# Odd chunks with hi and lo in each other's tile, so that successive moving operands of TensorE alternate between two offsets

## The chip, the core and the metric

The kernel runs on one core of a Trainium2 chip. The metric is the device time of one execution in microseconds (us), the median of several runs. TensorE is called PE here, VectorE DVE, ScalarE ACT, GpSimd POOL and SyncE SP, as in the profile.

## What is computed

Two layers of a diffusion backbone on 256 latent and 256 context tokens with 1024 features. Each layer is a gated feed-forward half step (FFN), a mixing step with four branches on one input projection, and a second FFN. Cut to what matters here:

```python
def ffn_half(z, shift, scale, gate, norm, wg, wu, wd):
    return z + 0.5 * gate * swiglu(modulate(rmsnorm(z, norm), shift, scale), wg, wu, wd)

def swiglu(z, wg, wu, wd):
    return (jax.nn.silu(z @ wg) * (z @ wu)) @ wd          # 1024 -> 2816 -> 1024

def merge_branches(branches, gate_pre, w_branch, w_out):
    gates = jax.nn.sigmoid(gate_pre).reshape(..., N_BRANCH, D_MODEL)
    merged = gates[..., 0, :] * (branches[0] @ w_branch[0])
    for n in range(1, N_BRANCH):
        merged = merged + gates[..., n, :] * (branches[n] @ w_branch[n])
    return merged @ w_out

for l in range(2):                                        # x: latent tokens, h: context tokens
    x = ffn_half(x, ...ffn1...); h = ffn_half(h, ...ffn1...)
    y, y_c = token_mixing(modulate(rmsnorm(x)), modulate(rmsnorm(h)), w_in[l], ...)
    x = x + mod[5] * y
    x = ffn_half(x, ...ffn2...)
    if l == 0: h = ffn_half(h + mod_c[5] * y_c, ...ffn2...)
return rmsnorm(x, final_norm)
```

All matrices are f32. The output is the latent stream, 256 x 1024.

## The kernel before

Activations lie with the features on the 128 partitions and the tokens along the free dimension: a tensor of 1024 features is 8 chunks of 128 partitions x 512 tokens (latent 0 to 255, context 256 to 511). Weights come in units of 128 x 1024 (8 blocks of 128 x 128).

Every large product is made of three fp32r matmuls. A value is split into hi, its fp32r rounding, and lo, the rest (`split`, L81 on ACT for hi, L84 on DVE for lo), and the product is hi x hi + hi x lo + lo x hi. `mm3` does this for a chunk k: L110 takes the weights' hi and the activations' hi, L111 the weights' hi and the activations' lo, L112 the weights' lo and the activations' hi. The activations are the moving operand (512 columns, or 256 where one half of the tokens is worked on), the weights the stationary one, loaded anew for each matmul. So the moving operands of a row of chunks run hi, lo, hi, hi, lo, hi. `group` (L123 to L125) does the same for several outputs side by side in the order hi, hi, lo, at the beginning of a phase. `proj_tok` (L615 to L617) has the activations as stationary operand.

The activations' parts lie in these tiles:

- `xs`, one tile for the whole kernel, holds hi (`xh`) and lo (`xl`) of the normed input of the current phase, 8 chunks of 2048 bytes a partition each. `place` puts them there by the table `PLACES`, in f32 elements: start of hi, distance of lo, and offsets `off` for the tiles below. In layer 0 and in the first FFN of layer 1 hi starts 60 elements into the tile and lo 8 x 512 + 32 further; as built, hi stands at 112 and lo at 240 bytes modulo 256. In the mixing and the second FFN of layer 1 the distance is 8 x 512, and both stand at 192.
- `hh` and `hl`, the FFN's hidden layer, 11 chunks of 2048 bytes each for one half of its 22 (`hidden`, by `off`): 112 and 240 modulo 256 in the same phases, both at 192 in the second FFN of layer 1.
- `bh` and `bl`, a branch's output (2 chunks), 112 and 240 in layer 0, one common offset in layer 1.
- `mh` and `ml`, the merged branches (8 chunks), at the beginning of their tiles: both at 0 in layer 0, both at 192 in layer 1.

The weight tiles `whi` and `wlo` stand at 0 modulo 256 nearly everywhere. The outputs' names tell the places: `pg` and `pu` are the FFN's first products, `pd` its second (11 chunks an output), `last` the last two outputs of a second product, made for 256 tokens at a time, `proj` the input projections, `gate` and `pb` the branches' gates and projections in `merge`, `po` the product with `w_out`, `mm`, `aux` and `first` those of `group`.

The tile framework sets each engine's order from the order in the code and from priorities; DMAs are issued by SP. A weight unit is loaded into `raw`, cast by ACT (`whi`), subtracted by DVE (`wlo`) and used by PE. In the last layer `early` (L396, L397) fills two columns of `xs` with the shift of the second FFN, hi by ACT and lo by DVE, while `merge` ends and `po` begins.

Of the kernel before, what the change touches and what calls it, by code (L numbers as in the profile page):

```python
# [10 lines left out]
F32 = mybir.dt.float32  # L11
F32R = mybir.dt.float32r
U8 = mybir.dt.uint8
AF = mybir.ActivationFunctionType
ALU = mybir.AluOpType
AX = mybir.AxisListType

P = 128
L = 2
D = 1024  # L20
NK = D // P
T = 256
TT = 2 * T
# [3 lines left out]
FH = NFC // 2  # L27
# [18 lines left out]
LINE = 32  # L46
# [2 lines left out]
PLACES = {(0, C_N1): (60, NK * TT + LINE, (28, 12)), (0, C_NM): (60, NK * TT + LINE, ((28, 60), (28, 60))),  # L49
          (0, C_N2): (60, NK * TT + LINE, (28, 12)), (1, C_N1): (60, NK * TT + LINE, (28, 12)),  # L50
          (1, C_NM): (80, NK * TT, ((0, 0), (64, 64))), (1, C_N2): (80, NK * TT, (112, 0))}


def ada_chunks(s):
# [4 lines left out]
class Net:  # L59
    def __init__(self, ctx, tc, ins, out):  # L60
        self.ctx, self.tc, self.nc, self.i, self.out = ctx, tc, tc.nc, ins, out
        self.n = 0
        pool = lambda name, **kw: ctx.enter_context(tc.tile_pool(name=name, **kw))
        self.cp = pool("const", bufs=1)
        self.wp = pool("weights", bufs=4)
        self.tp = pool("temps", bufs=2)
        self.ps = pool("psum", bufs=1, space=bass.MemoryType.PSUM)
        self.fill = self.apool = None
        self.steady, self.due = False, 0.0
# [113 lines left out]
    def place(self, l, phase):  # L183

        h, d, o = PLACES[l, phase]
        self.xh, self.xl = (self.xs[:, a:a + NK * TT].rearrange("p (k t) -> p k t", t=TT) for a in (h, h + d))
        return o

    def half(self):
# [199 lines left out]
    def early(self, l):  # L389


        nc = self.nc
        g = self.gain(l, 7, C_N2)
        sh = self.mods(l, 6)
        hi = self.xh[:, :, T - 2:T]
        nc.scalar.copy(hi, sh)  # L396
        nc.vector.tensor_tensor(out=self.xl[:, :, T - 2:T], in0=sh, in1=hi.bitcast(F32), op=ALU.subtract)  # L397
        return g

    def early_chunk(self, g, m):  # L400
# [65 lines left out]

    def hidden(self, hp, off):

        return tuple(hp.tile([P, FH * TT + pad], F32R, tag=t, name=t)[:, a:a + FH * TT].rearrange(
            "p (f t) -> p f t", t=TT) for t, pad, a in zip(("hh", "hl"), (112, 16), off))  # L470

    def cold_units(self, wgu, hp, evac, off):

# [369 lines left out]
    def mix(self, l, segs):  # L843
        nc, tc, i = self.nc, self.tc, self.i
# [3 lines left out]
        off = self.place(l, C_NM)  # L848
        with tc.tile_pool(name=f"mix{l}", bufs=1) as mp:
# [7 lines left out]
            turn = 1  # L857

            def branch():
                nonlocal turn  # L860
                turn = 1 - turn
                pair = [mp.tile([P, 2 * TT + 2 * LINE], F32R, tag=t, bufs=2, name=t) for t in ("bh", "bl")]
                return tuple(t[:, a:a + 2 * TT].rearrange("p (c t) -> p c t", t=TT) for t, a in zip(pair, off[turn]))

            def merge(b, bo, first=False):

                for m in range(NK):
                    if m % 4 == 0:
                        w = self.unit(i["wbr"][l, b, m // 4])
                    ps = self.mm("gate")  # L870
                    self.mm3(ps[:, :n], self.unit(i["wgate"][l, b, m]), self.xh, self.xl, range(NK), 0, n)
                    g = mp.tile([P, TT], F32, tag="g", bufs=2, name="g")
                    nc.scalar.activation(g[:, :n], ps[:, :n], AF.Tanh, scale=0.5)
                    ps = self.mm("pb")
                    self.mm3(ps[:, :n], w, bo[0], bo[1], (0, 1), 0, n, k0=2 * (m % 4))
                    t = acc[:, m, :n] if first else g[:, :n]
                    nc.vector.scalar_tensor_tensor(out=t, in0=g[:, :n], scalar=1.0, in1=ps[:, :n],
                                                   op0=ALU.add, op1=ALU.mult)
                    if not first:
                        nc.vector.tensor_tensor(out=acc[:, m, :n], in0=acc[:, m, :n], in1=t, op=ALU.add)  # L880
                    yield m
# [98 lines left out]
            with tc.tile_pool(name=f"br{l}", bufs=1) as bp:  # L980
# [66 lines left out]

                rounds(recurrence(0, obs))
                bc = branch()
                rounds(pooling(bc), "B")  # L1050
                ba = branch()
                rounds(attention_a(ba), "B")
                rounds(self.proj_tok(l, U_BI, bv))
                rounds(merge(2, bc, first=True))
                drain("B")
                rounds(recurrence(1, obs))
                drain("A")
                bd = branch()
                rounds(attention_d(bd))
                rounds(merge(0, ba))  # L1060
# [3 lines left out]
                bb = branch()  # L1064
                rounds(readout(bb))
            with tc.tile_pool(name=f"mg{l}", bufs=1) as gp:
                mh = gp.tile([P, NK, TT], F32R, tag="mh", name="mh")
                ml = gp.tile([P, NK, TT], F32R, tag="ml", name="ml")
                for m in merge(1, bb):
                    self.split(acc[:, m, :n], mh[:, m, :n], ml[:, m, :n])  # L1070
                gate = self.gate(l, 5)
                self.fresh(segs)
                g = self.early(l) if ns == 1 else None

                def out(m, ps, c0, c1, mid=iter(()), ws=[None] * NK):
                    if ws[m] is None:
                        ws[m] = self.unit(i["wout"][l, m], NK * P, *((gp, 2) if m >= NK - 2 else ()))
                    self.mm3(ps, ws[m], mh, ml, range(3), c0, c1, last=False)
                    next(mid, None)
                    self.mm3(ps, ws[m], mh, ml, range(3, 6), c0, c1, first=False, last=False, k0=3)  # L1080
                    next(mid, None)
                    self.mm3(ps, ws[m], mh, ml, range(6, NK), c0, c1, first=False, k0=6)

                for m in range(NK - 2):
                    ps = self.mm("po")
                    out(m, ps[:, :n], 0, n)
                    for r in segs:
                        self.update(ps, m, gate, r, r * T, True)
                    if g is not None:
                        self.early_chunk(g, m)  # L1090
                self.last_chunks(out, gate, segs, g)
# [163 lines left out]
```

## Time and profile before

| | us |
|---|---|
| median of 3 runs | 2109.31 |
| lowest and highest run | 2108.45, 2116.08 |
| the profiled execution | 2115.61 |
| its span, first to last instruction | 2113.8 |
| PE busy in it | 2087.5 |
| DVE busy | 1434.9 |
| ACT busy | 904.5 |

The granted clock of PE was 0.998 over the span. A row of a group of instructions names line, engine, operation, output and inputs, shape and count, then the busy time in us and the mean length of one in ns, then the idle time before them. A row of the timeline begins with the start in us from the span's start and the length in us. The ends of matmuls are modelled, and matmuls overlap; their starts are measured.

### The profile page before, as it was taken

The numbers are of one execution on the slowest core, as the hardware profiler recorded it, in microseconds if no ns is written. First come the engines' busy times: TensorE is split into PE (matmuls) and PEld (weight loads), VectorE is DVE, ScalarE is ACT, GpSimd is POOL, SyncE is SP. The second block draws the span as 40 slices with busy tenths as digits, with TensorE's granted clock in tenths as the row PEclk, the third lists the DMA queues.
The fourth block names the chain that finished last, engine by engine and source line by source line (L and its number), as shares of the span: only waits on it lengthen the run. The fifth ranks groups of instructions, "written<-read, shape, count | busy, mean of one in ns | idle before, by whom it ended". The sixth has DMA issues, their size and how long they took to land.

```text
span 2113.8 us, 31650 instructions
## 1 busy us (share of the span) xinstructions
PE 2087.5 (99%) x12446; PEld 1801.0 (85%) x12446; DVE 1434.9 (68%) x2355; ACT 904.5 (43%) x1488; POOL 39.4 (2%) x95
## 2 busy tenths in 40 slices
PE   8999999999999999999999999999999999999998
PEld 5888888988888888988888898888889989999998
DVE  5988986676366455676676667667666858677555
ACT  3332333547446433433233343223335655666443
POOL 0000000001000000000000000000000000000000
PEclk9999999999999999999999999999999999999999
DMA  7655654221222222344454334345443233455553
GB/s 304 216 175 188 215 186 140 96 98 51 75 76 80 71 97 98 110 143 138 144 183 157 124 128 161 130 156 173 146 128 114 98 120 110 141 184 181 176 189 116
DMA packets 89509, 296.71 MB, mean 140 GB/s; under 512 B 10256, under 2 KB 12176, under 8 KB 89360
## 3 DMA queue, kind: packets, MB, share of 16 engines
q1 hardware_dynamic: 89360, 294.69, 41.4%
q8 instruction: 98, 1.61, 0.3%
q14 instruction: 51, 0.42, 0.1%
HBM read 293.60 MB, written 1.05 MB: 139 GB/s over the span
## 4 chain that ended last, share of the span: by engine, by line
PE 94%; DVE 2%; ACT 2%; issue 1%; DMA 0%; DVEq 0%; ACTq 0%; SPq 0%
PE pg L110 6%; PE pu L110 6%; PE pg L112 6%; PE pu L112 6%; PE pg L111 6%; PE pu L111 6%; PE pd L110 6%; PE pd L112 6%; PE pd L111 6%; PE gate L112 4%; PE gate L110 4%; PE gate L111 4%; PE proj L111 2%; PE proj L110 2%; PE proj L112 2%; PE blev L777 2%
## 5 line engine op out<-in xcount | busy, mean ns | idle before, releaser
L81 ACT CAST whi<-raw 128x1024 fp32r<-128x1024 f32 (+2 forms) x444 | 430.7, 972 | 827.4 <-PE pu L111 200.3
L84 DVE TENSOR_TENSOR wlo<-raw,whi 128x1024 fp32r<-128x1024 f32 (+2 forms) x444 | 498.2, 1123 | 289.3 <-ACT whi L81 282.5
L285 DVE SCALAR_TENSOR_TENSOR aacc<-araw,sil,aacc 128x512 f32<-128x512 f32 x448 | 312.5, 745 | 122.0 <-DMA araw<-in_wada 121.6
L112 PE MATMUL pg<-xs,wlo 128*128 128x512 f32 (+1 forms) x640 | 233.0, 364 | 0.0
L112 PE MATMUL pu<-xs,wlo 128*128 128x512 f32 (+1 forms) x640 | 233.0, 364 | 0.0
L110 PE MATMUL pg<-xs,whi 128*128 128x512 f32 (+1 forms) x640 | 232.5, 363 | 0.4 <-ACT xs L376 0.4
L110 PE MATMUL pu<-xs,whi 128*128 128x512 f32 (+1 forms) x640 | 232.3, 363 | 0.0
L111 PE MATMUL pg<-xs,whi 128*128 128x512 f32 (+1 forms) x640 | 231.4, 362 | 0.0
L111 PE MATMUL pu<-xs,whi 128*128 128x512 f32 (+1 forms) x640 | 231.3, 361 | 0.0
L112 PE MATMUL pd<-hh,wlo 128*128 128x512 f32 (+1 forms) x616 | 224.3, 364 | 0.0
L110 PE MATMUL pd<-hh,whi 128*128 128x512 f32 (+1 forms) x616 | 223.8, 363 | 0.0
L111 PE MATMUL pd<-hl,whi 128*128 128x512 f32 (+1 forms) x616 | 222.7, 361 | 0.0
L110 PE MATMUL gate<-xs,whi 128*128 128x512 f32 (+1 forms) x512 | 172.5, 337 | 0.0
L112 PE MATMUL gate<-xs,wlo 128*128 128x512 f32 (+1 forms) x512 | 171.7, 335 | 0.0
L111 PE MATMUL gate<-xs,whi 128*128 128x512 f32 (+1 forms) x512 | 170.8, 334 | 0.0
L110 PEld LDWEIGHTS pg<-xs,whi 128*128 128x128 f32 x640 | 120.8, 189 | 20.8 <-issue 1.8
L110 PEld LDWEIGHTS pu<-xs,whi 128*128 128x128 f32 x640 | 120.8, 189 | 20.1 <-issue 2.0
L111 PEld LDWEIGHTS pu<-xs,whi 128*128 128x128 f32 x640 | 120.2, 188 | 19.4
L111 PEld LDWEIGHTS pg<-xs,whi 128*128 128x128 f32 x640 | 120.2, 188 | 19.4
L112 PEld LDWEIGHTS pg<-xs,wlo 128*128 128x128 f32 x640 | 120.1, 188 | 18.5
L112 PEld LDWEIGHTS pu<-xs,wlo 128*128 128x128 f32 x640 | 120.1, 188 | 18.5
L110 PEld LDWEIGHTS pd<-hh,whi 128*128 128x128 f32 x616 | 116.2, 189 | 19.5 <-issue 2.2
(278 smaller groups left out, 3794.5 us busy)
## 6 DMA issues: line engine op xcount, KB each, us to landing
raw<-in_wgu SPq DMA_DIRECT2D x176, 512.0 KB, 4.0
araw<-in_wada SPq DMA_DIRECT2D x128, 512.0 KB, 3.3
raw<-in_wgate SPq DMA_DIRECT2D x64, 512.0 KB, 3.2
raw<-in_wd SPq DMA_DIRECT2D x64, 384.0 KB, 3.1
raw<-in_win SPq DMA_DIRECT2D x44, 512.0 KB, 3.3
raw<-in_wd SPq DMA_DIRECT2D x64, 320.0 KB, 2.8
aspace<-in_wada SPq DMA_DIRECT2D x16, 512.0 KB, 8.9
raw<-in_wbr SPq DMA_DIRECT2D x16, 512.0 KB, 3.3
```

The costliest lines, as they stand in the source:

```text
L81: nc.scalar.copy(hi, src)
L84: nc.vector.tensor_tensor(out=lo, in0=src, in1=hi.bitcast(F32), op=ALU.subtract)
L110: nc.tensor.matmul(ps, wh, a, start=first and j == 0, stop=False)
L111: nc.tensor.matmul(ps, wh, b, start=False, stop=False)
L112: nc.tensor.matmul(ps, wl, a, start=False, stop=last and j == n - 1)
L285: nc.vector.scalar_tensor_tensor(out=acc[r], in0=w[:, j], scalar=c, in1=acc[r], op0=ALU.mult, op1=ALU.add)
L777: nc.tensor.matmul(ps[:, g * P:(g + 1) * P], k[:, h, g * P:(g + 1) * P], x[:, h, (g ^ cross) * P:((g ^ cross) + 1) * P], start=True, stop= ...
```

## The change

A new class `Chunks` holds two views of one shape and gives, for chunk i, the first where i is even and the second where it is odd. `parts(a, b)` makes two of them, with the views in one order and in the other. `place`, `hidden` and `branch` return such pairs, so that hi of an odd chunk lies where its lo lay, and lo where hi lay. `mh` and `ml` become such a pair too, and their tiles are 64 elements longer, with the offsets `off[0]` inside. `early`, which wrote all chunks in one instruction, writes even and odd chunks apart.

```diff
--- before.py
+++ after.py
@@ -49,6 +49,20 @@
 PLACES = {(0, C_N1): (60, NK * TT + LINE, (28, 12)), (0, C_NM): (60, NK * TT + LINE, ((28, 60), (28, 60))),
           (0, C_N2): (60, NK * TT + LINE, (28, 12)), (1, C_N1): (60, NK * TT + LINE, (28, 12)),
           (1, C_NM): (80, NK * TT, ((0, 0), (64, 64))), (1, C_N2): (80, NK * TT, (112, 0))}
+
+
+class Chunks:
+
+    def __init__(self, even, odd):
+        self.turns = (even, odd)
+
+    def __getitem__(self, i):
+        return self.turns[i[1] % 2][i]
+
+
+def parts(a, b):
+
+    return Chunks(a, b), Chunks(b, a)
 
 
 def ada_chunks(s):
@@ -183,7 +197,7 @@
     def place(self, l, phase):
 
         h, d, o = PLACES[l, phase]
-        self.xh, self.xl = (self.xs[:, a:a + NK * TT].rearrange("p (k t) -> p k t", t=TT) for a in (h, h + d))
+        self.xh, self.xl = parts(*(self.xs[:, a:a + NK * TT].rearrange("p (k t) -> p k t", t=TT) for a in (h, h + d)))
         return o
 
     def half(self):
@@ -392,9 +406,10 @@
         nc = self.nc
         g = self.gain(l, 7, C_N2)
         sh = self.mods(l, 6)
-        hi = self.xh[:, :, T - 2:T]
-        nc.scalar.copy(hi, sh)
-        nc.vector.tensor_tensor(out=self.xl[:, :, T - 2:T], in0=sh, in1=hi.bitcast(F32), op=ALU.subtract)
+        for j in range(2):
+            hi, lo = (x.turns[j][:, j::2, T - 2:T] for x in (self.xh, self.xl))
+            nc.scalar.copy(hi, sh[:, j::2])
+            nc.vector.tensor_tensor(out=lo, in0=sh[:, j::2], in1=hi.bitcast(F32), op=ALU.subtract)
         return g
 
     def early_chunk(self, g, m):
@@ -466,8 +481,8 @@
 
     def hidden(self, hp, off):
 
-        return tuple(hp.tile([P, FH * TT + pad], F32R, tag=t, name=t)[:, a:a + FH * TT].rearrange(
-            "p (f t) -> p f t", t=TT) for t, pad, a in zip(("hh", "hl"), (112, 16), off))
+        return parts(*(hp.tile([P, FH * TT + pad], F32R, tag=t, name=t)[:, a:a + FH * TT].rearrange(
+            "p (f t) -> p f t", t=TT) for t, pad, a in zip(("hh", "hl"), (112, 16), off)))
 
     def cold_units(self, wgu, hp, evac, off):
 
@@ -860,7 +875,7 @@
                 nonlocal turn
                 turn = 1 - turn
                 pair = [mp.tile([P, 2 * TT + 2 * LINE], F32R, tag=t, bufs=2, name=t) for t in ("bh", "bl")]
-                return tuple(t[:, a:a + 2 * TT].rearrange("p (c t) -> p c t", t=TT) for t, a in zip(pair, off[turn]))
+                return parts(*(t[:, a:a + 2 * TT].rearrange("p (c t) -> p c t", t=TT) for t, a in zip(pair, off[turn])))
 
             def merge(b, bo, first=False):
 
@@ -1064,8 +1079,8 @@
                 bb = branch()
                 rounds(readout(bb))
             with tc.tile_pool(name=f"mg{l}", bufs=1) as gp:
-                mh = gp.tile([P, NK, TT], F32R, tag="mh", name="mh")
-                ml = gp.tile([P, NK, TT], F32R, tag="ml", name="ml")
+                mh, ml = parts(*(gp.tile([P, NK * TT + 2 * LINE], F32R, tag=t, name=t)[:, a:a + NK * TT].rearrange(
+                    "p (k t) -> p k t", t=TT) for t, a in zip(("mh", "ml"), off[0])))
                 for m in merge(1, bb):
                     self.split(acc[:, m, :n], mh[:, m, :n], ml[:, m, :n])
                 gate = self.gate(l, 5)
```

Nothing moves on PE. In the second product of a first FFN (`pd`, layer 0; `hh` and `hl` are the two tiles, `whi` and `wlo` the weights' parts) the rows of PE before are these, three for a chunk, from an odd chunk on:

```order
L110 MATMUL pd<-hh,whi 128x512
L111 MATMUL pd<-hl,whi 128x512
L112 MATMUL pd<-hh,wlo 128x512
L110 MATMUL pd<-hh,whi 128x512
L111 MATMUL pd<-hl,whi 128x512
L112 MATMUL pd<-hh,wlo 128x512
```

and now, in the same place:

```order
L124 MATMUL pd<-hl,whi 128x512
L125 MATMUL pd<-hh,whi 128x512
L126 MATMUL pd<-hl,wlo 128x512
L124 MATMUL pd<-hh,whi 128x512
L125 MATMUL pd<-hl,whi 128x512
L126 MATMUL pd<-hh,wlo 128x512
```

In the odd chunk the two tiles have changed places, and no two rows that follow each other read the same one.

On ACT, where the last branch is merged in layer 1 and `po` begins (`g` is the Tanh of a gate, `mh` and `ml` the cast of a merged chunk, `whi` that of a weight unit, `xs<-mod_93` the copy in `early`), the rows before are:

```order
L81 CAST mh<-macc 128x256
L81 CAST whi<-raw 128x1024
L873 ACTIVATE g<-gate 128x256
L396 CAST xs<-mod_93 128x8x2
L81 CAST whi<-raw 128x1024
L81 CAST mh<-macc 128x256
```

and now:

```order
L95 CAST mh<-macc 128x256
L411 CAST xs<-mod_93 128x4x2
L95 CAST whi<-raw 128x1024
L888 ACTIVATE g<-gate 128x256
L411 CAST xs<-mod_93 128x4x2
L95 CAST whi<-raw 128x1024
L95 CAST ml<-macc 128x256
```

The copy of the even chunks stands one weight cast and one gate earlier than the whole copy stood; that of the odd chunks stands where it was. On DVE at the same place before:

```order
L84 TENSOR_TENSOR ml<-macc,mh 128x256
L84 TENSOR_TENSOR wlo<-raw,whi 128x1024
L877 SCALAR_TENSOR_TENSOR g<-g,pb 128x256
L397 TENSOR_TENSOR xs<-mod_93,xs 128x8x2
L84 TENSOR_TENSOR wlo<-raw,whi 128x1024
L880 TENSOR_TENSOR macc<-macc,g 128x256
```

and now:

```order
L98 TENSOR_TENSOR ml<-macc,mh 128x256
L412 TENSOR_TENSOR xs<-mod_93,xs 128x4x2
L98 TENSOR_TENSOR wlo<-raw,whi 128x1024
L892 SCALAR_TENSOR_TENSOR g<-g,pb 128x256
L412 TENSOR_TENSOR xs<-mod_93,xs 128x4x2
L98 TENSOR_TENSOR wlo<-raw,whi 128x1024
L895 TENSOR_TENSOR macc<-macc,g 128x256
```

Here too the first of the two subtracts has moved ahead of a weight unit and a gate.

## Rows read from the trace of the kernel before

**Rows 1.** The page: busy time (share) x instructions; the chain by engine.

```profile
PE 2087.5 (99%) x12446; PEld 1801.0 (85%) x12446; DVE 1434.9 (68%) x2355; ACT 904.5 (43%) x1488; POOL 39.4 (2%) x95
...
PE 94%; DVE 2%; ACT 2%; issue 1%; DMA 0%; DVEq 0%; ACTq 0%; SPq 0%
```

**Rows 2.** Groups of PE by shape, whole span: count | busy us, mean ns | idle.

```profile
L112 PE MATMUL pg<-xs,wlo 128*128 128x512 f32 x480 | 188.1, 392 | 0.0
...
L112 PE MATMUL pd<-hh,wlo 128*128 128x512 f32 x462 | 181.0, 392 | 0.0
...
L112 PE MATMUL gate<-xs,wlo 128*128 128x512 f32 x256 | 100.2, 392 | 0.0
...
L112 PE MATMUL proj<-xs,wlo 128*128 128x512 f32 x168 | 66.3, 395 | 0.0
...
L112 PE MATMUL pb<-bh,wlo 128*128 128x512 f32 x64 | 25.0, 391 | 0.0
...
L112 PE MATMUL po<-mh,wlo 128*128 128x512 f32 x48 | 18.7, 389 | 0.0
...
L827 PE MATMUL bctx<-bq,bk 128*128 128x256 f32 x32 | 7.5, 378 | 0.0
```

**Rows 3.** Timeline of PE, first FFN of layer 0: start us, length us, instruction.

```profile
73.31 0.39 PE L110 MATMUL pu<-xs,whi 128*128 128x512 f32 x1
...
84.20 0.39 PE L110 MATMUL pu<-xs,whi 128*128 128x512 f32 x1
```

**Rows 4.** Groups of PE by shape in the same stretch, 73.5 to 84.2 us.

```profile
L112 PE MATMUL pg<-xs,wlo 128*128 128x512 f32 x8 | 3.1, 391 | 0.0
...
L111 PE MATMUL pg<-xs,whi 128*128 128x512 f32 x8 | 3.1, 388 | 0.0
L110 PE MATMUL pg<-xs,whi 128*128 128x512 f32 x8 | 3.1, 387 | 0.0
```

**Rows 5.** Groups of PE in `po` of layer 0, 840 to 870 us.

```profile
L112 PE MATMUL po<-mh,wlo 128*128 128x512 f32 x45 | 17.5, 389 | 0.0
```

**Rows 6.** Timeline of PE in a 512-wide projection of layer 1.

```profile
1748.80 0.39 PE L110 MATMUL proj<-xs,whi 128*128 128x512 f32 x1
...
1753.00 0.39 PE L110 MATMUL proj<-xs,whi 128*128 128x512 f32 x1
```

**Rows 7.** Groups of PE in `last`, first FFN of layer 0, 386.5 to 395.5 us.

```profile
L111 PE MATMUL last<-hl,whi 128*128 128x256 f32 x27 | 7.5, 279 | 0.0
L112 PE MATMUL last<-hh,wlo 128*128 128x256 f32 x26 | 7.4, 284 | 0.0
L110 PE MATMUL last<-hh,whi 128*128 128x256 f32 x26 | 7.2, 275 | 0.0
```

**Rows 8.** The same, 398.8 to 402.4 us.

```profile
L110 PE MATMUL last<-hh,whi 128*128 128x256 f32 x11 | 3.1, 282 | 0.0
L112 PE MATMUL last<-hh,wlo 128*128 128x256 f32 x11 | 3.1, 279 | 0.0
L111 PE MATMUL last<-hl,whi 128*128 128x256 f32 x10 | 2.8, 279 | 0.0
```

**Rows 9.** Groups of PE in `gate` of layer 1, 1871.5 to 1874 us.

```profile
L110 PE MATMUL gate<-xs,whi 128*128 128x256 f32 x6 | 1.7, 276 | 0.0
```

**Rows 10.** The same, 1829.5 to 1832.5 us.

```profile
L110 PE MATMUL gate<-xs,whi 128*128 128x256 f32 x7 | 2.0, 281 | 0.0
```

**Rows 11.** Groups of PE in `last` of layer 0's mixing, 871 to 877.2 us.

```profile
L110 PE MATMUL last<-mh,whi 128*128 128x256 f32 x18 | 5.1, 283 | 0.0
```

**Rows 12.** Timeline of ACT around `early`: start, length, instruction, idle before and releaser.

```profile
1889.71 0.41 ACT L81 CAST mh<-macc 128x256 fp32r<-128x256 f32 x1 [1.80 <-DVE macc L880]
...
1891.25 0.20 ACT L396 CAST xs<-mod 128x16 fp32r<-128x16 f32 x1
1891.34 1.05 ACT L81 CAST whi<-raw 128x1024 fp32r<-128x1024 f32 x1
```

**Rows 13.** Timeline of PE a little later.

```profile
1894.71 0.38 PE L110 MATMUL po<-mh,whi 128*128 128x256 f32 x1 [0.28 <-ACT mh L81]
```

## Prediction

> **What bounds the kernel now.** The first view is the share of busy time and the chain that ended last [rows 1]: TensorE (PE) is busy 99% of the span, and 94% of the chain is its matmuls; VectorE (DVE) and ScalarE (ACT) stand at 68% and 43%. So the time is the number of matmuls times their spacing, and a change of spacing passes through almost whole. The second view is the matmul groups by line and shape [rows 2]. The 512-column chunks of `mm3` (L110, L111, L112: hi, lo, hi of the activations) are the bulk: 480 chunks in `pg`, 480 alike in `pu`, 462 in `pd`, 256 in `gate`, 168 in `proj`, 64 in `pb`, 48 in `po`. All but `po` (48 chunks) and the 48 `proj` chunks of layer 1 read hi at 112 and lo at 240 modulo 256, so 1,862 chunks, 5,586 matmuls, are what the change is about.
>
> The third view is how far apart those matmuls start. A recorded length is not that spacing: ends are modelled, and a length outlasts the distance to the next start by about 162 ns. In a stretch of pure stream, 16 chunks take from 73.31 to 84.20 us [rows 3], that is 0.680 us a chunk or 226.7 ns a matmul. The lengths in that stretch [rows 4] split it: L110 387, L111 388, L112 391, so spacings of 225, 226 and 229 ns. The 229 is the step from L112 of a chunk to L110 of the next, the only one of the three in which two successive moving operands have the same offset.
>
> **The change part by part.**
>
> *The 512-wide chunks.* The instructions, their order on PE and their weights stay; in odd chunks hi and lo stand in each other's place, and the offsets run 112, 240, 112, 240 without a repeat. Only from the last, even chunk of an eleven-chunk unit of `pd` to the next unit does the repeat stay (42 units). Of 1,862 repeats about 1,800 go. Read as prices, the spacings say: 391 less the mean of 387 and 388 is 3.5 ns, times 1,800 is 6.3 us off. I don't take that, for three reasons.
> First, `po` in layer 0 has both operands at one offset (0), so every step there is a repeat, and its three lengths are 389 each ([rows 5]; the rows of L110 and L111 there read alike): 3 x 227 = 681 ns a chunk, the same as 225 + 226 + 229 = 680. A stream of nothing but repeats is no slower than one with a repeat in three.
> Second, the 256-wide `last` chunks have the same offsets and the same order. Early in one such stage the lengths are 275, 279, 284 [rows 7], so spacings 113, 117, 122; some microseconds on, in the next output chunks, they are 282, 279, 279 [rows 8]: the repeat is now among the short steps and the first alternating one the long step. The sums are 838 and 840, equal within rounding. So a spacing is not the price of a pair of offsets. What is kept is the sum over a chunk, and the three starts only shift inside it.
> Third, 680 ns for 1,536 columns is 0.443 ns a column, and the fastest 256-wide stream comes to the same: 276 - 162 = 114 ns [rows 9], 0.445 a column. Two widths and three placements end at one rate, which looks like a floor of the stream.
> I take 0 for this term. Its bounds: below, the 6.3 us; above, the worst 512-wide stream of the trace, `proj` in layer 1 with both operands at offset 192, 6 chunks from 1748.80 to 1753.00 us [rows 6], 0.700 us a chunk: 20 ns more, times 1,862 is 37 us.
>
> The Trainium skill, "TensorE: Matmul & The Clock Gate", section "Step-by-step: what each phase is for", says that loading the next weights has a read port of its own and takes no SBUF read bandwidth from the running matmul. By that rule an offset could change nothing between two reads of PE, and both bounds would be 0. The trace agrees only in part: one offset or another does give 0.680 or 0.700 us a chunk [rows 3, 6].
>
> *`mh` and `ml`.* In layer 0 they get the two offsets. The 48 `po` chunks are at 681 already: 0. The 32 `last` chunks that read them have lengths of 283 [rows 11], 849 a chunk, where the alternating `last` chunks have 838: 11 x 32 = 0.4 us off, if that carries over. In layer 1 the two parts keep one common offset, as `xs`, `bh` and the second FFN's `hh` there do, and swapping them changes no offset at all.
>
> *The other 256-wide chunks.* By the code these are the 132 `last` chunks on `hh` with two offsets, 176 in the opening groups of three phases (hi, hi, lo there, so repeats stay and only trade places), and 64 in `proj_tok` of layer 0, where the swapped parts are stationary: 372 in all. The same tiles at one fixed offset run at lengths of 276 or 281 [rows 9, 10] with nothing different in the instructions, and 283 is the worst [rows 11]; against the 279 mean of [rows 7] that is -10 to +11 ns a chunk, so -3.7 to +4.1 us. I take 0, since nothing says which of these rates a stretch falls into.
>
> *`early`.* One copy on ACT and one subtract on DVE become two of each. The copy of 16 columns takes 0.20 us and delays the next start by 0.09 [rows 12]. In the ACT queue the first half now stands ahead of a weight cast and of the last gate's Tanh, with a wait for PE; PE's read that it waits for ends before ACT has finished the `mh` cast ahead of it (1889.71 + 0.41), so it does not hold the queue up. Behind the Tanh, DVE makes the last `macc` and ACT the last `mh`, and there PE already waits 0.28 us [rows 13]. So up to 0.1 to 0.2 us lands on PE, once; I take 0.2. DVE's extra subtract stands in the same chain and is in that figure. No DMA and no other queue moves.
>
> *Sum.* 0 - 0.4 + 0 + 0.2 = -0.2 us. The profiled execution took 2115.61 us (span 2113.8); the median of the runs shown is 2109.31, 6.3 us lower, and the difference has nothing to do with the change. Taken off the median: 2109.1 us.
>
> **The rivals.**
>
> *The repeats do cost 3.5 ns each* (a gain): 2109.1 - 6.3 = 2102.8 us. For it: the split in [rows 4] is steady over the stretch. Against it: [rows 5] and the pair [rows 7, 8].
>
> *The stream loses its fast footing* (slower): the repeat in every third step may be what lets a stream settle at 0.680 after each wait. Without it the 112/240 chunks could run as the layer-1 `proj` chunks do, at 0.700 [rows 6]: 2109.1 + 37 = 2146 us. It decides as soon as the mean chunk passes 685.7 ns, since 10.5 us / 1,862 is 5.7 ns. For it: such streams exist at the same width, and [rows 9, 10] show two rates for one placement. Against it: `po`, which has no alternation at all, sits at 681, and 112 and 240 each stand at the fast rate now.
>
> *The floor is no floor*: a plain-f32 matmul of 256 columns has 378 - 162 = 216 ns a record (the `bctx` row of [rows 2]), 0.844 a column, just twice 0.422, as if the array's step were 0.422 ns and not 0.443. If what the fp32r stream loses against that were lost at repeats, the 5,586 matmuls would gain 226.7 - 216 = 10.7 ns each: 60 us, 2049 us. Against it: the alternating steps of [rows 4] are at 225 and 226, not 216. The Trainium skill's page "TensorE: Matmul & The Clock Gate", section "Back-to-back issue gap", gives N/2.4 + 2.5 ns, 215.7 at 512 columns; by that the gain would be this rival's, and no fp32r stream of this trace is that fast.
>
> *The swap does not alternate.* In the second FFN and the mixing of layer 1 it cannot, as said; elsewhere the built order shows it. This would give the forecast's time.
>
> **How the numbers follow.** Forecast 80%, repeats priced 8%, lost footing 10%, no floor 2%. A measurement of this kernel can tell about 0.5% (10.5 us) from no change. Forecast and the first rival lie within it, so: faster 0.03, same 0.87, slower 0.10. The likeliest case by itself reaches from -3.7 - 0.4 to +4.1 + 0.2 us about 2109.3, so from 2105.2 to 2113.6; at the upper end stands also what the executions of the unchanged kernel do by themselves (2108.45 to 2116.08). Down to the first rival and up to those executions, the range is 2102 to 2117; the lost footing and the lost floor are left out, 12 in 100.
>
> **What would show it.** Right: the chunks of `pg` and `pd` still start 0.680 us apart, with three lengths that are now alike, near 389; `po` unchanged; `last` on `hh` with a sum near 838. The first rival: lengths of 387 and 388 at all three lines and 0.676 us a chunk. The second: lengths of 393 and more and 0.69 to 0.70. The third: lengths near 378. The step on which all rests is that the sum over a chunk and not the pair of offsets is what the hardware keeps; an unbroken 225/226 would refute it.

## The result

| | before | after |
|---|---|---|
| median, us | 2109.63 (4 runs) | 2126.84 (4 runs) |
| lowest and highest | 2108.45, 2116.08 | 2124.89, 2132.14 |
| profiled execution, its span | 2115.61, 2113.8 | 2127.04, 2125.3 |

The changed kernel is slower: ratio 1.0083, 95% interval 1.0068 to 1.0099, 17.2 us by the medians. The forecast was no change, 2102 to 2117.

The executions of either kernel fall into two groups, 5 to 7 us apart, and the profile of before is from the upper one, that of after from the lower. That comes from layer 1 and is told of further down; below, lower group stands against lower and upper against upper. The granted clock is 0.998 in both profiles.

### The profile page after: what moved, and what is told of

The parts are those of the page before. It is cut to its first block, busy times and chain, and to the rows that moved or that the text cites. A ratio compares the mean times of both kernels' runs of the same rounds, so it can differ in the third digit from the quotient of the medians.

```text
span 2125.3 us, 31654 instructions
## 1 busy us (share of the span) xinstructions
PE 2099.3 (99%) x12446; PEld 1796.3 (85%) x12446; DVE 1437.2 (68%) x2356; ACT 905.7 (43%) x1489; POOL 39.3 (2%) x95
## 4 chain that ended last, share of the span: by engine, by line
PE 94%; DVE 3%; ACT 2%; issue 1%; DMA 0%; DVEq 0%; ACTq 0%
PE pg L124 6%; PE pu L124 6%; PE pg L126 6%; PE pu L126 6%; PE pg L125 6%; PE pu L125 6%; PE pd L124 6%; PE pd L126 6%; PE pd L125 6%; PE gate L124 4%; PE gate L126 4%; PE gate L125 4%; PE proj L125 2%; PE proj L124 2%; PE proj L126 2%; PE blev L792 2%
## 5 line engine op out<-in xcount | busy, mean ns | idle before, releaser
L126 PE MATMUL pg<-xs,wlo 128*128 128x512 f32 (+1 forms) x640 | 232.8, 364 | 0.0
L126 PE MATMUL pu<-xs,wlo 128*128 128x512 f32 (+1 forms) x640 | 232.7, 364 | 0.0
L126 PE MATMUL gate<-xs,wlo 128*128 128x512 f32 (+1 forms) x512 | 172.2, 336 | 0.0
L126 PEld LDWEIGHTS pu<-xs,wlo 128*128 128x128 f32 x640 | 120.2, 188 | 20.3
L126 PEld LDWEIGHTS pg<-xs,wlo 128*128 128x128 f32 x640 | 120.2, 188 | 20.3
L124 PE MATMUL pd<-hh,whi 128*128 128x512 f32 (+1 forms) x336 | 122.8, 365 | 0.0
L125 PE MATMUL pd<-hl,whi 128*128 128x512 f32 (+1 forms) x336 | 122.3, 364 | 0.0
L126 PE MATMUL pd<-hh,wlo 128*128 128x512 f32 (+1 forms) x336 | 122.0, 363 | 0.0
L124 PEld LDWEIGHTS gate<-xs,whi 128*128 128x128 f32 x512 | 96.4, 188 | 11.6 <-issue 0.9
```

Source lines behind the costliest of these rows:

```text
L124: nc.tensor.matmul(ps, wh, a, start=first and j == 0, stop=False)
L125: nc.tensor.matmul(ps, wh, b, start=False, stop=False)
L126: nc.tensor.matmul(ps, wl, a, start=False, stop=last and j == n - 1)
```

## The profile after

The page of the changed kernel: busy time of PE and the chain.

```profile
PE 2099.3 (99%) x12446; PEld 1796.3 (85%) x12446; DVE 1437.2 (68%) x2356; ACT 905.7 (43%) x1489; POOL 39.3 (2%) x95
...
PE 94%; DVE 3%; ACT 2%; issue 1%; DMA 0%; DVEq 0%; ACTq 0%
```

Against [rows 1] only PE has grown; its waits are the same. Two starts of L126 from the timeline, in the stretch that answers to [rows 3], 16 chunks apart:

```profile
74.09 0.40 PE L126 MATMUL pu<-xs,wlo 128*128 128x512 f32 x1
...
85.14 0.40 PE L126 MATMUL pu<-xs,wlo 128*128 128x512 f32 x1
```

11.05 / 16 = 0.691 us a chunk, where [rows 3] had 0.680. The groups by shape in that stretch (73.5 to 84.2 us), against [rows 4]:

```profile
L124 PE MATMUL pg<-xs,whi 128*128 128x512 f32 x8 | 3.1, 392 | 0.0
L125 PE MATMUL pg<-xs,whi 128*128 128x512 f32 x8 | 3.1, 392 | 0.0
L126 PE MATMUL pg<-xs,wlo 128*128 128x512 f32 x8 | 3.1, 392 | 0.0
```

387, 388, 391 have become 392, 392, 392. The three are alike, as the forecast said, but at 230 ns apart and not at 227: 10 ns a chunk, 18.6 us if all 1,862 chunks pay it. Over the whole trace the distances from start to start in these chunks, waits between them included, grew by 16 us. A second reading shows why the two spans differ by 11.5 us only. The 256-wide `pg` of layer 1, whose places the change does not touch, before and then after:

```profile
L112 PE MATMUL pg<-xs,wlo 128*128 128x256 f32 x160 | 45.0, 281 | 0.0
```

```profile
L126 PE MATMUL pg<-xs,wlo 128*128 128x256 f32 x160 | 44.2, 276 | 0.0
```

281 less 276, times three, is 15 ns a chunk by these rounded lengths and 13 by the starts (353 and 340), and `pg`, `pu` and `pd` of that phase have 160 + 160 + 154 chunks: 6 to 7 us by which this execution of before was the slower one for a reason of its own.

## The experiments

**Streams by themselves.** A program that keeps only the matmuls, 32 chunks a stream, with hardly any work on other engines (shortened; `h` and `l` are the places of hi and lo):

```python
for k in range(NK):
    h, l = a + k * TT, lo + k * TT
    if alt and k % 2:
        h, l = l, h
    for w, m in ((wh, h), (wh, l), (wl, h)):
        nc.tensor.matmul(ps[:, :n], w, xs[:, m:m + n], ...)
```

> This program leaves the model's computation out altogether and runs only streams of fp32r matmuls, three a chunk, 96 a stream, each with one arrangement of the two activation parts; its time says nothing, only the chunk time of each stream counts. The output is named by width (wide 512, half 256 columns), arrangement (rep: hi, lo, hi in every chunk, one repeated tile in three; alt: the two parts swapped in odd chunks, no repeat) and the two places modulo 256 bytes (a 0, b 16, c 32, d 48, e 64, g 96, h 112, i 128, m 192, p 240); _w has the weights at 64 and not 0. Theory A, a repeat anchors the stream: every stream in which an offset comes twice in a row settles at 680 ns a chunk (hp rep, hh, pp, aa, ai rep), and both that alternate without a repeat, hp alt and ai alt, at 690. Theory B, each place has a rate of its own and a stream is their mix: of hh and pp one is at 680 or below and the other near 700, so that hp rep (two thirds of one, one third of the other) and hp alt (half and half) come out different; ai alt lies between aa and ii. Theory C, alternation costs only where a row begins inside a 128-byte line: hp alt 690, ai alt 680, hh and pp alike. The forecast's own reason, a rate that the stream keeps whatever the order: 680 in all but the m streams, which are at 700. For 256 columns the same with 340 (the fastest seen), 345 to 353 where alternation costs, and the mm stream at 340 or 353.

Groups of PE by stream, both passes of each together; a chunk is twice the `whi` length plus the `wlo` length less 3 x 162 ns. The lengths are rounded, so this can be 2 ns off; where the text has another number, it is from the starts:

```profile
L61 PE MATMUL wide_rep_pp<-xs,whi 128*128 128x512 f32 x128 | 40.3, 396 | 0.0
...
L61 PE MATMUL wide_rep_hh<-xs,whi 128*128 128x512 f32 x128 | 40.1, 394 | 0.0
...
L61 PE MATMUL wide_alt_hp<-xs,whi 128*128 128x512 f32 x128 | 39.8, 392 | 0.0
...
L61 PE MATMUL wide_alt_ai<-xs,whi 128*128 128x512 f32 x128 | 39.8, 392 | 0.0
...
L61 PE MATMUL wide_rep_aa<-xs,whi 128*128 128x512 f32 x128 | 39.4, 389 | 0.0
L61 PE MATMUL wide_rep_hp<-xs,whi 128*128 128x512 f32 x128 | 39.3, 388 | 0.0
...
L61 PE MATMUL wide_rep_pp<-xs,wlo 128*128 128x512 f32 x64 | 25.3, 396 | 0.0
...
L61 PE MATMUL wide_alt_hp<-xs,wlo 128*128 128x512 f32 x64 | 25.1, 392 | 0.0
L61 PE MATMUL wide_alt_ai<-xs,wlo 128*128 128x512 f32 x64 | 25.1, 392 | 0.0
L61 PE MATMUL wide_rep_hp<-xs,wlo 128*128 128x512 f32 x64 | 25.0, 391 | 0.0
...
L61 PE MATMUL wide_rep_hh<-xs,wlo 128*128 128x512 f32 x64 | 24.9, 390 | 0.0
L61 PE MATMUL wide_rep_aa<-xs,wlo 128*128 128x512 f32 x64 | 24.9, 389 | 0.0
```

By that formula the arrangement of before (`rep_hp`) is at 681, that of after (`alt_hp`) at 690; the starts say 680 and 690. So the loss is in PE's own stream and needs nothing beside PE. Theory A falls: `hh` and `pp` are nothing but repeats and stand at 693 and 700. B falls: two thirds of 693 and one third of 700 is 695, and `rep_hp` is at 680. C falls: `alt_ai`, with places that begin a 128-byte line, is at 690 too. Of the 512-wide streams only `aa` and `rep_hp` are at 680. One stream, `rep_ai`, ran at 687 when it came first and at 700 when the program came to it again.

**One part of the swap at a time.** In the first kernel only `place` uses `parts`, in the second only `hidden`; nothing else is swapped. The longer `mh` and `ml` tiles of the change stay in both, and `early` in two halves in the first. Against before, cut to the lines that count:

```diff
-        self.xh, self.xl = (self.xs[...] for a in (h, h + d))
+        self.xh, self.xl = parts(*(self.xs[...] for a in (h, h + d)))
```

```diff
-        return tuple(hp.tile(...) for t, pad, a in zip(("hh", "hl"), (112, 16), off))
+        return parts(*(hp.tile(...) for t, pad, a in zip(("hh", "hl"), (112, 16), off)))
```

> Only xh and xl are swapped in odd chunks; hidden, branch, mh and ml are as before. If the loss is the alternation in whichever stream has it (A, B and C alike), it follows the chunks: pg, pu, gate and proj rose by 4.2 + 4.2 + 2.2 + 0.9 = 11.5 us of the 17 in the trace of the changed kernel, so about 2121 us, with pd back at 0.680 us a chunk. If the loss needs both swaps, or came from another part of the edit (early, the longer mh and ml tiles), it stays at 2109 to 2112 or shows in pd as well.

> Only hh and hl are swapped in odd chunks; xs, branch, mh, ml and early are as before. By the chunks: pd rose by 4.0 us, and the 256-wide last chunks on hh by up to 0.7, so 2113 to 2114.5 us, with pg, pu and gate at 0.680 us a chunk. If the swaps are not additive, 2109 or above 2117.

`xs` alone: 2120.9 us in the lower group and 2126.7 to 2127.6 in the upper, where before, on the same chip, had 2108.4 to 2109.5 and 2115.1 to 2117.2: 11 to 12 us more (1.0051, 1.0029 to 1.0072, groups mixed). `hh` alone: 2113.3 to 2114.7 and 2119.5 to 2121.4, 4 to 5 more (1.0014, 0.9998 to 1.0030). L126 in `pd` of the first FFN, ten chunks apart, first with `xs` alone and then with `hh` alone:

```profile
169.90 0.39 PE L126 MATMUL pd<-hh,wlo 128*128 128x512 f32 x1
...
176.70 0.39 PE L126 MATMUL pd<-hh,wlo 128*128 128x512 f32 x1
```

```profile
170.15 0.39 PE L126 MATMUL pd<-hh,wlo 128*128 128x512 f32 x1
...
177.05 0.39 PE L126 MATMUL pd<-hl,wlo 128*128 128x512 f32 x1
```

680 and 690 ns a chunk. Each stream has its own loss, and the two add up to 15 to 17 of the 17 us.

**The repeat put back.** The swap stays; in odd chunks `mm3` takes lo first:

```diff
+            one, two = (b, a) if k % 2 else (a, b)
-            nc.tensor.matmul(ps, wh, a, start=first and j == 0, stop=False)
-            nc.tensor.matmul(ps, wh, b, start=False, stop=False)
+            nc.tensor.matmul(ps, wh, one, start=first and j == 0, stop=False)
+            nc.tensor.matmul(ps, wh, two, start=False, stop=False)
```

> The whole swap stays, but mm3 takes lo first in odd chunks: the places then run 112, 240, 112, 112, 240, 240, so each place is read as often as in the changed kernel and one step in three is a repeat again. Theory A, a repeat anchors the stream: the 512-wide chunks return to 680 ns and the time to 2109 us (within 3). Theory B, the mix of places sets the time: it stays at 2127 us and the chunks at a mean of 690. Theory C as A or B, it does not tell here. The forecast's reason alone (the order does not matter) has fallen with the result; a part of A that held only for a repeat of one of the two places would show as 685 a chunk and 2118.

2130.95 us in the lower group, 2138.0 to 2139.6 in the upper (1.0111, 1.0084 to 1.0138): not back at 2109 but 22 us above it. L126 is L127 here; twenty chunks from about 150 us on:

```profile
149.30 0.39 PE L127 MATMUL pg<-xs,wlo 128*128 128x512 f32 x1
...
163.16 0.39 PE L127 MATMUL pd<-hl,wlo 128*128 128x512 f32 x1
```

693 ns a chunk. A repeat in every third step is no anchor. The order of the same two places, 112 240 112, 112 240 112 240 or 112 240 112 112 240 240, gives 680, 690 or 693.

**The weights' place.** Beside the running matmul PE loads the next one's weights: these loads (PEld) fill 85% of the span in the page above, the matmuls 99%. A second program of streams varies the weights' place, and a kernel shifts them by 64 bytes; `pad` moves them, and `pad2`, 192 bytes behind them, leaves all that follows where it was modulo 256:

```diff
         self.wp = pool("weights", bufs=4)
+        pool("pad", bufs=1).tile([P, 48], F32, name="pad2")
...
         self.fb = cp.tile([P, L, 4], F32, name="fb")
+        cp.tile([P, 16], F32, name="pad")
```

> Again only streams of matmuls, with the model's computation left out; names as in the first such program, and behind them the place of the weights modulo 256 bytes (wa 0, wb 16, and so on to wp 240), mid and thin for 64 and 32 weight columns and not 128, same for one and the same weight block in every matmul, back for the order of the whole kernel with the repeat put back. Theories A to C have fallen (a stream of repeats alone runs at 680, 693 or 700 by its place, a repeat put back made the kernel slower). Theory D: PE's own reads of the weights and of the activations meet, and what counts is the place of the one against the other. Then shifting both by the same amount changes nothing: aa_wa, ee_we, ii_wi, mm_wm all 680 ns a chunk; hh_wa, ll_we, pp_wi, dd_wm all 693; pp_wa, dd_we, hh_wi, ll_wm all 700; rep ld_we, ph_wi, dl_wm 680 and their alt 690; the streams of 112 and 240 change with the weights' place (rep_hp_we 693, as once before); and with 64 or 32 weight columns, where less is read, the differences between places shrink to under half. Theory E: only the activations' places and their order count: all sixteen rep_hp streams stay at 680 and all alt_hp at 690, the shifted pairs follow their activations (dd, ll, pp alike whatever the weights), and narrow weights change nothing. Under either, back_hp is at 693 to 694, as in the whole kernel.

> The kernel before, nothing swapped; the weights' tiles lie 64 bytes further, so that nine tenths of the stationary operands stand at 64 and not at 0 modulo 256. Theory D: the 512-wide chunks of 112 and 240 go from 680 to 693 ns as in the stream with such weights, 0.9 x 1,862 x 13 = 22 us, so 2131 us, or 2138 where the 256-wide streams of layer 1 run at 353. Theory E: 680 ns a chunk still, 2109 to 2116 us.

One tile of the streams each: shortest, median and longest length in ns, then the first and the last start; 31 chunks lie between these two.

```profile
L66 PE MATMUL wide_rep_aa_wa<-xs,wlo x32: 388/389/397, 737.0 to 758.1; 128*128 128x512 f32 x32
...
L66 PE MATMUL wide_rep_mm_wm<-xs,wlo x32: 388/389/397, 802.4 to 823.5; 128*128 128x512 f32 x32
...
L66 PE MATMUL wide_rep_hh_wa<-xs,wlo x32: 387/387/395, 824.2 to 845.7; 128*128 128x512 f32 x32
...
L66 PE MATMUL wide_rep_dd_wm<-xs,wlo x32: 387/387/395, 890.8 to 912.3; 128*128 128x512 f32 x32
...
L66 PE MATMUL wide_alt_dl_wm<-xs,wlo x32: 388/391/393, 1113.3 to 1134.7; 128*128 128x512 f32 x32
...
L66 PE MATMUL wide_rep_hp_wj<-xs,wlo x32: 388/388/388, 426.8 to 447.9; 128*128 128x512 f32 x32
...
L66 PE MATMUL wide_alt_hp_wj<-xs,wlo x32: 388/389/397, 448.6 to 469.7; 128*128 128x512 f32 x32
...
L66 PE MATMUL wide_rep_hp_wb<-xs,wlo x32: 387/395/395, 71.2 to 92.9; 128*128 128x512 f32 x32
...
L66 PE MATMUL wide_alt_hp_wb<-xs,wlo x32: 392/392/395, 93.6 to 115.0; 128*128 128x512 f32 x32
...
L66 PE MATMUL wide_rep_hp_we<-xs,wlo x32: 387/394/397, 205.1 to 226.6; 128*128 128x512 f32 x32
...
L66 PE MATMUL wide_alt_hp_we<-xs,wlo x32: 387/392/403, 227.3 to 248.7; 128*128 128x512 f32 x32
```

`mm` ran at 700 in the first program, with the weights at 0, and `dd` too. Here, with the weights shifted as far as they, `mm_wm` takes 21.1 us and `dd_wm` 21.5, just as `aa_wa` and `hh_wa` (680 and 693 ns a chunk); the two pairs between them, and `ld_we`, `ph_wi`, `dl_wm` (680, and 690 alternating), do the same. Each of them settles anew: `mm_wm` needs 684 to 697 ns for each of its first four chunks, then 680. So a shift of both by 64, 128 or 192 bytes changes nothing; a shift of the weights alone changes most rates. With the weights at 144 both arrangements run at 680 (`wj`), with no repeat in the second; at 16 the swap gains, 21.7 to 21.4 us, 700 to 690 (`wb`), and at 64 from 696 to 690 (`we`). Of the sixteen places of the weights, two gave 680 to the old arrangement and one to the new; the rest lie between 685 and 700.

The kernel with the shifted weights took 2144.49 us (1.0159, 1.0140 to 1.0179), 35 us more with not one activation moved modulo 256. Theory E has fallen. D said 22 us, or 29 with layer 1 in its upper group; the remainder is in layer 1's 256-wide chunks, with lengths of 281 to 282 where the lower group has 276, and in chunks at 694 to 696 where the sum had 693.

One expectation of D was missed: with 64 weight columns the spread of the five arrangements was 680 to 699 and with 32 it was 680 to 695, against 680 to 710 with 128; none is under half. But the narrower weights change which arrangement is fast: unswapped 687 and swapped 680 at either width, where 128 columns have 680 and 690. One and the same weight block in every matmul gave the rates of eight different ones, and the order of the repeat put back gave 693, as in the kernel. No stream fell below 680 with narrow weights either, so nothing here shows the loading of weights as what limits a stream at its best.

**The swap at other places.** If the price hangs on the places, the same swap must cost something else elsewhere. First the changed kernel with its two places moved, then the swap with the weights 64 further, then the unswapped kernel at the moved places (the first of the changed lines; the other places go the same way):

```diff
-PLACES = {(0, C_N1): (60, NK * TT + LINE, (28, 12)), (0, C_NM): (60, NK * TT + LINE, ((28, 60), (28, 60))),
+PLACES = {(0, C_N1): (88, NK * TT + LINE, (56, 40)), (0, C_NM): (88, NK * TT + LINE, ((56, 24), (56, 24))),
```

> The changed kernel, swap and alternation as they are, with the two activation places of layer 0 and of layer 1's first FFN at 224 and 96 and not at 112 and 240 modulo 256; the weights stay at 0. Measured against the weights this is the pair 112 and 240 with weights at 144, and of that stream both arrangements ran at 680. If the place against the weights decides: the 512-wide chunks run at 680 with no repeat in them, and the time is that of the kernel before, 2109 us or 2116 in its two groups, give or take 1.5 us for the 256-wide chunks whose price at these places is not known. If alternation as such costs: 690 a chunk and 2127 us.

> The swap as in the changed kernel, with the weights 64 bytes further (nine tenths of them at 64). The same weights without the swap gave 2144.5 us and 694 to 696 ns a chunk. If alternation as such costs 10 ns a chunk wherever the operands lie, 2144.5 + 17 = 2161 us. If the price of the swap hangs on the places, the stream with weights at 64 decides (alternating 690.7 ns, twice; unswapped 693 and 696): the swap is then a gain of 3 to 5 ns a chunk here, 0.9 x 1,862 x 4.3 = 7 us, so 2137 us.

> The kernel before, nothing swapped, with the two places at 224 and 96 as in the run before last; the swapped one took 2147.2 us, with 698 to 700 ns a chunk. If alternation as such costs 10 ns a chunk, this one is at 2147 - 17 = 2130 us, at 690. If the places decide, the stream says 700 (unswapped), so 2109 + 1,862 x 0.020 = 2146 us, and the swap changes nothing there.

The first missed by 38 us: 2147.19 (1.0170, 1.0153 to 1.0188), 695 to 700 ns a chunk. Moving the activations by -144 bytes is not the same as moving the weights by +144; the equality above was seen for steps of 64 only. So theory D, the place of the one against the other, is not the whole rule. Streams of the next program, at 224 and 96:

```profile
L66 PE MATMUL wide_rep_og_wa<-xs,wlo x32: 389/397/397, 925.6 to 947.3; 128*128 128x512 f32 x32
...
L66 PE MATMUL wide_alt_og_wa<-xs,wlo x32: 392/395/397, 948.0 to 969.5; 128*128 128x512 f32 x32
```

21.7 and 21.5 us, 700 and, by the starts, 695 a chunk. The other two came as expected: 2137.03 (1.0122, 1.0103 to 1.0141) and 2146.61 (1.0167, 1.0146 to 1.0189). Twenty chunks from about 150 us on, weights 64 further, unswapped and then swapped:

```profile
149.58 0.40 PE L113 MATMUL pg<-xs,wlo 128*128 128x512 f32 x1
...
163.51 0.40 PE L113 MATMUL pd<-hh,wlo 128*128 128x512 f32 x1
```

```profile
149.22 0.40 PE L127 MATMUL pg<-xs,wlo 128*128 128x512 f32 x1
...
163.02 0.40 PE L127 MATMUL pd<-hh,wlo 128*128 128x512 f32 x1
```

697 and 690 ns. So one and the same swap costs 17 us at 112 and 240. It gains 7 us where the weights lie 64 bytes further (2144.5 to 2137.0; the kernel before, run beside each, began at 2108.2 and 2108.4). At 224 and 96 it changes little: the lower executions are at 2142.9 and 2143.1 without it and at 2140.5 with it, the others at 2146.6 to 2148.9 and 2146.4 to 2148.1. In unbroken stretches of 512-wide chunks both kernels are at 699; the 695 of the bare stream is not met in the kernel.

**All places, and layer 1.**

> Streams of matmuls alone, the model's computation left out; names as before. The 256-wide streams of 112 and 240 with the weights at each of sixteen places, then each single place against weights at 0 for both widths. By theory D the single places repeat what they gave (wide aa 680, hh 693, pp 700 to 710, mm 700; half hh 340, aa 360, mm 353), 224 and 96 give 680 in both arrangements at 512 columns, and the spread over places is of the same kind at 256 columns, between 340 and about 363, with no arrangement below 340. A place that gives 680 for 512 and 340 for 256 columns would be the best for this kernel; if there is none, no swap of places can beat the kernel before by more than its 256-wide chunks, about 5 us.

At 512 columns `aa` gave 680 again and `hh` 693; `pp` gave 680 here, where it had 700 in the first program and 710 in the second. At 256 columns `hh` was at 340, `aa` at 360, and `mm`, at 353 in the first program, at 340 here:

```profile
L66 PE MATMUL half_rep_mm_wa<-xs,wlo x32: 276/276/277, 880.4 to 890.9; 128*128 128x256 f32 x32
```

So some streams have more than one rate for one arrangement of places, and keep the one in which they settle. That what ran ahead decides is likely: within the first program it is all that is known to differ between the two passes of `rep_ai` (687 and 700). Between programs more differs, the weights' tiles among it. No stream beat 680 or 340, and no pair of places that was run at both widths gave both. That fits the two groups: layer 1 stands at 192, `mm`, and its `pg`, `pu` and `pd` are at 353 ns in every trace of the upper group (before, `xs` alone, the swap at 224 and 96) and at 340 in every trace of the lower (after, `hh` alone, the repeat put back, 224 and 96 unswapped). The last kernel moves its places to 112, with nothing swapped (one of the changed lines; the tiles of `hl`, `mh` and `ml` grow with it):

```diff
-          (1, C_NM): (80, NK * TT, ((0, 0), (64, 64))), (1, C_N2): (80, NK * TT, (112, 0))}
+          (1, C_NM): (60, NK * TT, ((44, 44), (44, 44))), (1, C_N2): (60, NK * TT, (28, 44))}
```

> The kernel before, nothing swapped; in the mixing and the second FFN of layer 1 all activation parts stand at 112 and not at 192 modulo 256 (hi and lo alike). The executions of the kernel before fall into two groups, 2108 to 2109.5 and 2115 to 2117 us; their traces say that the 256-wide chunks of layer 1 then run at 340 or at 353 ns, with the same instructions. The stream of 256 columns at 112 ran at 340 both times, that at 192 at 353. If the place decides, all executions fall together at about 2106 us: the gate, pb, po and last chunks that are at 345 to 360 even in the lower group come to 341 (about 2 us), and the 48 projections at 512 columns from 700 to 693 (0.3 us). If something else decides between the two modes, two groups remain, 7 us apart.

2107.91 us, eleven runs from 2107.50 to 2108.20, where before had 2108.16 to 2116.04 beside it: 0.9987 (0.9978 to 0.9996), faster than both kernels, and one group. Only three of the fifteen executions of before beside it were in the upper group, so eleven without one point to the place without proving it. The gain on the lower group is 1 us and not the 2 to 3 expected; `gate` came down as expected (276 and 277 for 279 in two of its three rows), the 16 `last` chunks on `mh` stayed near 358.

## Why the prediction was wrong

*The bulk.* Where the time is, and that a change of spacing passes through almost whole, held: 17 us out of 10 ns times 1,862. The step that failed is the term of the 512-wide chunks, taken as 0 between -6.3 and +37; it is +16, at 690 ns a chunk in place of 680. It rested on the rule that the sum over a chunk is kept whatever the order of the two places, and the swap by itself, in a bare stream, changes that sum. Of the three reasons for it:

- `po` [rows 5] is a stream of repeats at 681. That is the rate of place 0 with the weights at 0 (`aa`), not the rate of repeats: `hh` and `pp` are repeats as well, at 693 and 700.
- "What is kept is the sum over a chunk" was read off [rows 7] and [rows 8], which share one order of places and differ only in where they came in. The sum is kept as long as the order of places is. The swap makes another order, and the rows could not speak for it.
- 0.443 ns a column held as the lowest rate seen: no stream here was under 680 or 340. But it is the best of what a stream may do, not what it returns to.

*The rivals.* The lost footing was the right direction at half the price, 0.690 and not 0.700; its mechanism, the repeat as anchor, fell with the repeat put back. The cheaper steps among the alternating ones (225 and 226 in [rows 4]) were no price of a pair, as the forecast said: an unbroken alternation came to 230 and 230.

*A read port of its own.* "TensorE: Matmul & The Clock Gate", section "Step-by-step: what each phase is for", in the Trainium skill, gives the weights' load a read port of its own that takes nothing from the running matmul. The forecast found it half borne out; the runs go against it: the weights' place alone moved the stream from 680 to 693 and more, and the kernel by 35 us, and with the activations shifted as far the stream was back at 680 (`ld_we`), so it is not the weights' place by itself. That "their weights stay" was said in passing, as if that settled their part.

*The small terms.* `po` rose from 389 to 390 and 395 with the two places, half a microsecond that was forecast as 0. In layer 0 the `last` chunks on `mh` fell from 360 to 353 ns, a gain as forecast (0.2 us for 0.4), and those on `hh` rose from 353 to 358. `early` left no new wait on PE. None of these decided anything. The 0.80 for no change was too much, since all three reasons rested on rows of other places or of the order before.

What stays open is the inner cause: that PE's two reads hinder each other is argued from places, and no run looks inside. Nor do the runs say why one order of two places settles at 680 and another at 690. They show that the places of both operands and their order decide, for some streams together with something that came before, and that no other engine is needed for it.

## What to carry to other kernels

Where PE is the bound and each matmul loads new weights, the places of both operands modulo 256 bytes and the order in which they are read can set the rate of the stream: 3% lay between the best and the common places here. A tuned kernel may stand on one of few good places, so a change of layout or order that moves no instruction needs a stream of its own, measured with the weights where they are, before it is taken as free. A rate read off one order is no evidence for another.

## What the runs showed of the hardware

- fp32r streams of 512 columns settle between 680 and 710 ns for three matmuls, of 256 columns between 340 and 360, by places, order and what came before, at a granted clock of 0.999 to 1.0.
- Shifting weights and activations together by 64, 128 or 192 bytes left the rate as it was to 1 ns in the five arrangements tried; shifting the activations of 112 and 240 by -144 or the weights by +144 is not the same (700 and 680).
- One arrangement can have several rates (`pp`: 680, 700, 710; `rep_ai`: 687, 700; 256-wide `mm`: 340, 353), each kept through the stream once it has settled. In this kernel the two rates of the 256-wide chunks are worth 7 us from one execution to the next.
